# Decoder layer on one core: half of x and the first weights on two queues, and the first four weight chunks applied to both token blocks before their norm factors are known

## The chip, the cores and the metric

The kernel runs on one core of a Trainium2 chip. The metric is the device time of one execution in microseconds (us), as the median of several runs. A profile of one execution gives, per engine, when each instruction ran: PE multiplies matrices (PEld is its loading of the stationary operand), DVE is the vector engine, ACT the scalar engine, POOL is GpSimd, and SP issues transfers.

## The reference

One hybrid decoder layer over x of 256 tokens by 1024 channels, in float32. What matters here is its first sub-layer:

```python
h = h + 0.5 * rmsnorm(swiglu(rmsnorm(h, ffn1_pre_g), ffn1_w_gate, ffn1_w_up, ffn1_w_down), ffn1_post_g)
# rmsnorm(x, g) = x * rsqrt(mean(x*x) + EPS) * g
# swiglu(u)     = (silu(u @ w_gate) * (u @ w_up)) @ w_down
```

Behind it stand a Mamba-2 branch and a differential attention branch beside each other, their gated merge, and a second sub-layer of the same kind. The norm factor r = rsqrt(...) is one number per token, so that it can be applied to a token's row before or after a product with the weights: (r x g) W = r (x g W).

## The kernel before, in words

**Precision.** Every float32 operand of a product is split in two: hi is the operand cast to a rounded 32-bit form, lo is what the cast lost. A product is hi·hi + lo·hi + hi·lo, so each pair of 128-wide tiles costs three matmuls. ACT makes hi (line 167 for weights, 343 and 191 for activations) and DVE makes lo (168, 345, 192).

**Weights** come in chunks of 1 MB through three `raw` buffers (`load_to`, line 140). SP issues the transfers. A buffer is loaded again once DVE has made the last lo of the chunk in it. The first chunk is loaded in four pieces of 256 KB and split in four pieces; chunks 1 to 3 are loaded in halves. `take()` hands out the next split chunk and sees to it that chunks ahead are split.

**Tokens** are two blocks of 128 (block 0 and 1). For a product, x must be transposed (channels on partitions): PE transposes four 128x128 tiles into one PSUM tile `pu`, ACT and DVE read it, multiply by the gain column g, and write hi and lo.

**The start** (lines 263 to 612). ACT issues the transfer of the gain (`stage_f`), SP those of x in four quarters (block 0 halves 0 and 1, block 1 halves 0 and 1), then the weights. PE does six warm-up matmuls (`WARM`) on an identity matrix, transposes the gain (299), transposes both halves of block 0 (340), and does eight more warm-up matmuls (`FILL`). Block 0 goes unscaled, as x·g, into `raw_u`. Block 1 is scaled first: DVE sums its squares (364), POOL makes r1 (330, 331) and multiplies x by it (`un_f`, 373), PE transposes `un_f`, and ACT and DVE write the scaled `u_f`.

**The four first chunks** are w_gate and w_up for the first 512 hidden columns, halves of 512 channels each. `Norm.products` (484) goes through the products (block 0, gate), (block 1, gate), (block 0, up), (block 1, up), two chunks each, twelve matmuls of 128x512 per chunk and block (`mm_nat`, 222), 96 in all. Block 0's results get r0 when they leave PSUM (`evict`, 524). Later products need block 0 scaled too: POOL makes a diagonal matrix of r0 (`dr_f`, 378), PE multiplies it by ones so that r0 stands on every row (`rb_f`, 385), ACT copies that (387), DVE makes the scaled x (`us_f`, 392), and ACT and DVE split it into `u_f` (191, 192). `back` (533) transposes the finished 512 columns of a block (`pt_f`, 537).

**The order.** Inside `own_order` (from line 264 to the `free_order` at the end of `products`) PE, ACT, DVE and SP run in the order in which the program is written; POOL is placed by the scheduler. Behind it the scheduler places all of them. From chunk 4 on (`mm_w`, 206: `pg_f`, `pup_f`) the products are of both blocks at a time.

Of the kernel before, what the change touches and what calls it, by code (L numbers as in the profile page):

```python
# [15 lines left out]
F32R = mybir.dt.float32r  # L16
# [20 lines left out]
RAW_BUFS = 3  # L37
AHEAD = 3
WARM = 6
FILL = 8  # L40
TAIL = 3
BG_US = 3.15
GATE_US = 1.35
# [5 lines left out]
def tile_hybrid_layer(ctx: ExitStack, tc: tile.TileContext, x, ffn1_pre_g, ffn1_w_gate, ffn1_w_up,  # L49
# [19 lines left out]
    def jk(shape, name):  # L69
        return sb.tile(shape, F32, tag="jk", name=name, bufs=2)  # L70
# [12 lines left out]
    def bg(shape, name):  # L83
        return ps.tile(shape, F32, tag="bg", name=name, bufs=5)
# [137 lines left out]
    def mm_nat(acc, w, act, k0, first, last, late):  # L222
# [7 lines left out]
        for i, ((a, b), j) in enumerate(terms):  # L230
            nc.tensor.matmul(acc, a(k0 + j), b(j), start=first and i == 0, stop=last and i == 11)  # L231
# [54 lines left out]
    ones = const.tile([P, P], F32, name="ones")  # L286
    nc.gpsimd.memset(ones, 1.0)

    pw = bg([P, P], "warm")

    def warm(n):

# [2 lines left out]

    warm(WARM)
    cols_f = const.tile([P, KD], F32, name="cols_f")
    pt = bg([P, KD], "pt_cols_f")
    nc.tensor.transpose(pt, stage_f, ident[:KD, :KD])
    nc.vector.tensor_copy(cols_f, pt)  # L300
    cols_a = const.tile([P, P], F32, name="cols_a")
# [31 lines left out]
        return r  # L333

    last_pool = [None]
    def turn(b, q, src, g, to, name):

        pu = bg([P, 4, P], f"pu_{name}{b}{q}")
        for i in range(4):
            nc.tensor.transpose(pu[:, i, :], src[:, i * P:(i + 1) * P], ident)  # L340
        hi, lo = to(q)
        for i in range(4):
            nc.scalar.activation(hi[:, i, :], pu[:, i, :], AF.Identity, scale=g(q * 4 + i))
        for i in range(4):
            nc.vector.scalar_tensor_tensor(lo[:, i, :], pu[:, i, :], g(q * 4 + i), hi[:, i, :].bitcast(F32),
                                           ALU.mult, ALU.subtract)
        return pu

    def in_u(b):
# [8 lines left out]
    def rms(b, tag, eng=None):  # L358

        ss = tiny(2, f"ss_{tag}{b}")  # L360
        for q in range(2):
            src = h[:, b, halves[q]]
            if eng is nc.vector:
                nc.vector.scalar_tensor_tensor(jk([P, 512], f"sq_{tag}{b}{q}"), src, 1.0 / D, src, ALU.mult,
                                               ALU.mult, accum_out=ss[:, q:q + 1])
            else:
                sum_sq(ss[:, q:q + 1], src, 1.0, f"sq_{tag}{b}{q}")
        return rstd_of(ss, 1.0, f"r_{tag}{b}")

    def unit(b, q, r, tag, eng):  # L370
# [7 lines left out]
        last_pool[0] = nc.gpsimd.tensor_scalar(dr, ident, r, None, ALU.mult).ins  # L378
        return dr

    def rescaled(pus, r, g, tag, dr):

        dr = diag(r, tag) if dr is None else dr
        rb = bg([P, P], f"rb_{tag}")
        nc.tensor.matmul(rb, ones, dr, start=True, stop=True)
        rbs = k2([P, P], f"rbs_{tag}")
        nc.scalar.copy(rbs, rb)
        out = []
# [8 lines left out]
    def set_u(us):  # L397
        for q in range(2):
            split(*in_u(0)(q), us[q])

    def post_norm(b, acc, pg, fold, tag):

# [55 lines left out]
    class Norm:  # L458
# [3 lines left out]
        def __init__(self, tag, g):  # L462
            self.tag, self.g, self.pus = tag, g, []
            new_u(tag)
            self.to0 = in_u(0)
            self.dr = None
            self.left = []

        def block0(self):
# [7 lines left out]
        def unit1(self, engs=(nc.vector, nc.vector)):  # L477
            r = rms(1, self.tag)
            self.un = [unit(1, q, r, self.tag, engs[q]) for q in range(2)]

        def turn1(self, q):
            turn(1, q, self.un[q], self.g, in_u(1), self.tag)

        def products(self, ws, evict, at, turns=((0, 0), (0, 1), (1, 0), (1, 1)), late="u"):

            n = 0
            for b, i in turns:
                act = of_block(self.to0 if b == 0 else in_u(1))  # L490
                acc = pj(f"pn_{self.tag}{b}{i}")
                for c in range(2):
                    mm_nat(acc, ws[2 * i + c], act, c * 4, c == 0, c == 1, late if b == 0 else "u")
                    n += 1
                    for f in at.get(n, ()):
                        f()
                if b == 1:
                    evict(b, i, acc, None)
                else:
                    self.left.append(lambda i=i, acc=acc: evict(0, i, acc, self.r0))  # L500
            free_order()

        def turns1(self):
# [7 lines left out]
            self.left.clear()  # L511

        def rescale(self):
            set_u(rescaled(self.pus, self.r0, self.g, self.tag, self.dr))

    def ffn(post_v, tag, norm, ready, turned, then, at, ws=None, **kw):
# [23 lines left out]
        norm.products(ws or [take(1) for _ in range(4)], evict,  # L540
                      {n: [f if f else lambda: back(0) for f in fs] for n, fs in at.items()}, **kw)
# [24 lines left out]


    norm = Norm("f1", lambda j: cols_f[:, j:j + 1])
    raw_u = [k4([P, 4, 2, P], f"raw_u{q}", F32R) for q in range(2)]
    norm.to0 = lambda q: (raw_u[q][:, :, 0, :], raw_u[q][:, :, 1, :])  # L570
    norm.r0 = rms(0, "f1")
    r1 = rms(1, "f1", nc.vector)
    norm.un = [unit(1, q, r1, "f1", nc.gpsimd) for q in range(2)]
    norm.dr = diag(norm.r0, "f1")
    norm.turn0(0)
    for _ in split_steps(False):
        pass
    norm.turn0(1)
    warm(FILL)
    load_to(1 + RAW_BUFS)  # L580

    def gains():
        after_start.append(last_pool[0])
# [9 lines left out]
    def next_norm(tag, name):  # L593
# [9 lines left out]

        return made, ready, lambda: made[0].block0()

    ws = [take(1) for _ in range(2)]
    more = lambda: ws.append(take(1))
    made, ready, turned = next_norm("mx", "mx")
    ffn(ffn1_post_g, "f1", norm, ready, turned, gains,
        {1: [norm.turns1], 2: [more], 4: [norm.settle, more], 5: [norm.rescale], 7: [norm.settle, None]}, ws,  # L610
        turns=((0, 0), (1, 0), (0, 1), (1, 1)), late="w")
    norm = made[0]


# [47 lines left out]
    norm.products([take(1) for _ in range(4)], evict_v,  # L662
                  {3: [norm.turns1], 5: [norm.settle, norm.rescale]})
# [484 lines left out]
    ffn(ffn2_post_g, "f2", norm, store, lambda: None, lambda: None,  # L1148
        {3: [norm.turns1], 5: [norm.settle, norm.rescale], 7: [None]})

    free_order()

# [31 lines left out]
```

## Time and profile before

Median 753.45 us of 3 runs (753.43 to 754.12). The profiled execution took 753.31 us, of which the span from its first to its last instruction is 751.6 us.

| engine | busy us | share of the span |
|---|---|---|
| PE | 742.0 | 99% |
| PEld | 643.8 | 86% |
| DVE | 522.1 | 69% |
| ACT | 437.9 | 58% |
| POOL | 41.0 | 5% |

The granted clock of PE is 0.999 on average. The time from 0 to about 35 us is the start and the four first chunks; it is the only part that the change touches. PE's busy share says that matmuls were in flight, not that they followed each other as closely as they can, so the stage is read from the start times of its rows.

### The profile page before, as it was taken

What the parts mean: (1) busy time and instruction counts of PE and PEld (TensorE: products, weight loads), DVE (VectorE), ACT (ScalarE), POOL (GpSimd) and SP (SyncE); (2) the same over time, 40 slices, a digit from 0 to 9 for tenths busy, and PEclk for the clock granted to TensorE, in tenths of its full rate; (3) what the DMA queues carried; (4) which work ended last, traced back from release to release, by engine and by line L of the source; (5) the groups of instructions that cost most, each with busy time, mean ns of one, the idle gap of its engine ahead of it and who ended that gap; (6) DMA issues with size and microseconds to landing.
All of it is one profiled execution on the core that took longest, in us unless ns stands there. A gap on an engine that the chain in (4) does not pass through costs nothing.

```text
span 751.6 us, 11066 instructions
## 1 busy us (share of the span) xinstructions
PE 742.0 (99%) x4385; PEld 643.8 (86%) x4385; DVE 522.1 (69%) x790; ACT 437.9 (58%) x731; POOL 41.0 (5%) x76
## 2 busy tenths in 40 slices
PE   8999999999999999999999999999999999999996
PEld 7888888888889999898999778788888888888885
DVE  6685667654577888868777987696684867766612
ACT  7475556643565565858867555783563756664511
POOL 7400000000200000000000000000010000000000
PEclk9999999999999999999999999999999999999999
DMA  8685666486253647565556454376371777544701
GB/s 316 158 276 162 222 224 240 181 280 223 64 168 115 203 135 242 169 200 183 161 168 202 166 192 152 129 230 246 112 232 49 225 223 224 177 176 184 275 1 56
DMA packets 94212, 137.96 MB, mean 184 GB/s; under 512 B 2684, under 2 KB 68304, under 8 KB 94160
## 3 DMA queue, kind: packets, MB, share of 16 engines
q1 hardware_dynamic: 91488, 129.51, 52.3%
q0 software_dynamic: 2368, 7.22, 3.2%
q8 instruction: 34, 0.56, 0.3%
q10 hardware_dynamic: 304, 0.53, 0.2%
q14 instruction: 18, 0.15, 0.1%
HBM read 136.17 MB, written 1.08 MB: 183 GB/s over the span
## 4 chain that ended last, share of the span: by engine, by line
PE 96%; DVE 1%; POOL 1%; DMA 1%; ACT 1%; issue 0%; SPq 0%; DVEq 0%; POOLq 0%; ACTq 0%
PE acc_f L433 16%; PE pup_f L216 9%; PE pg_f L216 9%; PE pws L231 6%; PE pgt L231 6%; PE pn_f L231 5%; PE pg_f L215 4%; PE pup_f L215 4%; PE acc_mx L433 3%; PE pn_mx L231 3%; PE pwd L231 3%; PE pxs L204 2%; PE pxs L202 2%; PE pxs L201 2%; PE pz L204 2%; PE pz L201 2%
## 5 line engine op out<-in xcount | busy, mean ns | idle before, releaser
L168 DVE TENSOR_TENSOR wlo<-raw,whi 128x1024 fp32r<-128x1024 f32 (+1 forms) x246 | 291.6, 1213 | 53.6 <-ACT whi L167 50.9
L167 ACT CAST whi<-raw 128x1024 fp32r<-128x1024 f32 (+1 forms) x246 | 247.3, 1044 | 56.7 <-PE acc_f L433 22.7
L216 PE MATMUL pg_f<-u_f,whi 128*128 128x512 f32 x288 | 101.2, 396 | 0.0
L216 PE MATMUL pup_f<-u_f,whi 128*128 128x512 f32 x288 | 101.1, 396 | 0.0
L215 PE MATMUL pg_f<-u_f,wlo 128*128 128x256 f32 x252 | 70.5, 280 | 0.0
L215 PE MATMUL pup_f<-u_f,wlo 128*128 128x256 f32 x252 | 70.3, 279 | 0.0
L216 PEld LDWEIGHTS pg_f<-u_f,whi 128*128 128x128 f32 x288 | 52.9, 188 | 9.8
L216 PEld LDWEIGHTS pup_f<-u_f,whi 128*128 128x128 f32 x288 | 52.7, 188 | 9.8
L433 PE MATMUL acc_f<-whi,gh_f 128*128 128x512 f32 x176 | 58.2, 390 | 0.0
L433 PE MATMUL acc_f<-wlo,gh_f 128*128 128x512 f32 x176 | 58.1, 389 | 0.0
L433 PE MATMUL acc_f<-whi,gl_f 128*128 128x512 f32 x176 | 58.1, 389 | 0.0
L215 PEld LDWEIGHTS pg_f<-u_f,wlo 128*128 128x128 f32 x252 | 47.5, 188 | 1.7
L215 PEld LDWEIGHTS pup_f<-u_f,wlo 128*128 128x128 f32 x252 | 47.5, 189 | 1.6
L220 DVE TENSOR_TENSOR su_f<-pup_f,su_f 128x256 f32<-128x256 f32 x36 | 15.2, 422 | 40.5 <-ACT su_f L219 40.5
L433 PEld LDWEIGHTS acc_f<-wlo,gh_f 128*128 128x128 f32 x176 | 33.0, 188 | 6.9
L433 PEld LDWEIGHTS acc_f<-whi,gl_f 128*128 128x128 f32 x176 | 33.0, 188 | 6.8
L433 PEld LDWEIGHTS acc_f<-whi,gh_f 128*128 128x128 f32 x176 | 33.0, 188 | 6.8
L231 PE MATMUL pgt<-whi,u_mx 128*128 128x512 f32 x128 | 34.8, 400 | 0.0
L201 PE MATMUL pz<-u_mx,whi 128*128 128x256 f32 x128 | 32.3, 288 | 0.0
L219 ACT COPY su_f<-pup_f 128x256 f32<-128x256 f32 x36 | 13.4, 371 | 32.2 <-PE pup_f L216 32.1
L202 PE MATMUL pz<-u_mx,whi 128*128 128x256 f32 x128 | 31.8, 284 | 0.0
L201 PE MATMUL pxs<-u_mx,whi 128*128 128x256 f32 x128 | 31.7, 285 | 0.0
(310 smaller groups left out, 1435.9 us busy)
## 6 DMA issues: line engine op xcount, KB each, us to landing
raw<-in_w_in_dram SPq DMA_DIRECT2D x40, 1024.0 KB, 5.4
raw<-in_ffn_w_down_dram SPq DMA_DIRECT2D x22, 1024.0 KB, 5.0
raw<-in_ffn_w_gate_dram SPq DMA_DIRECT2D x20, 1024.0 KB, 5.7
raw<-in_ffn_w_up_dram SPq DMA_DIRECT2D x20, 1024.0 KB, 5.5
raw<-in_ssd_w_branch_dram SPq DMA_DIRECT2D x8, 1024.0 KB, 5.1
acb<-acd POOLq DMA_DIRECT2D x8, 512.0 KB, 4.9
raw<-in_da_w_branch_dram SPq DMA_DIRECT2D x4, 1024.0 KB, 5.1
raw<-in_w_out_dram SPq DMA_DIRECT2D x4, 1024.0 KB, 5.0
```

The lines of the kernel that those rows point to most:

```text
L167: nc.scalar.copy(hi[:, js, :], r[:, q * nj + j:q * nj + j + n, :])
L168: nc.vector.tensor_sub(lo[:, js, :], r[:, q * nj + j:q * nj + j + n, :], hi[:, js, :].bitcast(F32))
L201: nc.tensor.matmul(acc[m], wh(j)[:, cs], ah(k0 + j), start=first and j == ks[0], stop=False)
L202: nc.tensor.matmul(acc[m], wh(j)[:, cs], al(k0 + j), start=False, stop=False)
L204: nc.tensor.matmul(acc[m], wl(j)[:, cs], ah(k0 + j), start=False, stop=last and j == ks[-1])
L215: nc.tensor.matmul(acc[:, :T], wl(j)[:, cs], ah(j), start=False, stop=False)
L216: nc.tensor.matmul(acc, wh(j)[:, cs], ahl(j), start=j == 0, stop=j == KD - 1)
L219: nc.scalar.copy(dst[:, m, :], acc[:, T:])
L220: nc.vector.tensor_tensor(dst[:, m, :], acc[:, :T], dst[:, m, :], ALU.add)
L231: nc.tensor.matmul(acc, a(k0 + j), b(j), start=first and i == 0, stop=last and i == 11)
L433: nc.tensor.matmul(acc[b][q], x_[:, ts], w_(kt)[:, halves[q]], start=i == 0 and kt == 0 and x_ is ah and w_ is wh, stop=i == n - 1 and kt ...
```

## The change

Constant `FILL` goes from 8 to 2. ACT's queue now issues the first halves of x of both blocks, behind the gain; SP issues the first weight chunk in its four pieces, then the second halves of x, then the other weights. `WARM` and its place stay.

Neither block is scaled before the product: both are transposed unscaled into `raw_u`. A new `mm_both` multiplies one chunk with both blocks, k-tile by k-tile, hi pieces first; all four chunks go through it in the order gate 0, gate 1, up 0, up 1. Both blocks get r when they leave PSUM, and both get the way over `dr_f`, `rb_f`, `rbs`, `us_f` and `u_f`. The squares of block 0 are summed on DVE, those of block 1 on ACT. Two of the four transposes of x, and one of the two `rb_f`, are put between matmuls of a chunk.

```diff
-FILL = 8
+FILL = 2
...
+    def mm_both(accs, w, acts, k0, first, last, between={}):
+        wh, wl = w
+        his = [[(b, a, wh, j) for b in range(2) for a in acts[b]] for j in range(4)]
+        los = [[(b, acts[b][0], wl, j) for b in range(2)] for j in range(4)]
+        terms = his[0] + his[1] + los[0] + his[2] + los[1] + his[3] + los[2] + los[3]
+        for i, (b, x_, w_, j) in enumerate(terms):
+            nc.tensor.matmul(accs[b], x_(k0 + j), w_(j), start=first and j == 0 and w_ is wh and x_ is acts[b][0],
+                             stop=last and j == 3 and w_ is wl)
+            if i + 1 in between:
+                between[i + 1]()
...
     for b in range(2):
-        for q in range(2):
-            nc.sync.dma_start(h[:, b, halves[q]], xv[:, b, halves[q]])
+        nc.scalar.dma_start(h[:, b, halves[0]], xv[:, b, halves[0]])
+    load_to(1)
+    for b in range(2):
+        nc.sync.dma_start(h[:, b, halves[1]], xv[:, b, halves[1]])
     load_to(RAW_BUFS)
...
-    norm.r0 = rms(0, "f1")
-    r1 = rms(1, "f1", nc.vector)
-    norm.un = [unit(1, q, r1, "f1", nc.gpsimd) for q in range(2)]
-    norm.dr = diag(norm.r0, "f1")
-    norm.turn0(0)
-    for _ in split_steps(False):
-        pass
-    norm.turn0(1)
-    warm(FILL)
+    square(ss_f[0], 0, 0, "f1", nc.vector)
+    raised(0, 0)
+    warm(FILL)
+    raised(1, 0)
+    raw(0, 0)
+    steps = split_steps(False)
+    next(steps)
+    raw(1, 0)
+    for _ in steps:
+        pass
     load_to(1 + RAW_BUFS)
...
+    def first_products(evict, back):
+        acts = [of_block(to) for to in raw_to]
+        acc = [[pj(f"pn_f1{b}0") for b in range(2)], None]
+        mm_both(acc[0], take(1), acts, 0, True, False, {16: lambda: raised(0, 1), 20: lambda: raised(1, 1)})
+        square(ss_f[0], 0, 1, "f1", nc.vector)
+        r = [rstd_of(ss_f[0], 1.0, "r_f10")]
+        dr = diag(r[0], "f10")
+        raw(0, 1)
+        raw(1, 1)
+        rb = bg([P, 2, P], "rb_f1")
+        rbs = []
+        w = take(1)
+        rbs.append(on_rows(rb[:, 0, :], dr, "f10"))
+        for q in range(2):
+            square(ss_f[1], 1, q, "f1")
+        r.append(rstd_of(ss_f[1], 1.0, "r_f11"))
+        us = rescaled(pus[0], rbs[0], gain_f, "f10")
+        dr = diag(r[1], "f11")
+        w2 = take(1)
+        mm_both(acc[0], w, acts, 4, False, True, {16: lambda: rbs.append(on_rows(rb[:, 1, :], dr, "f11"))})
+        set_u(0, us)
+        acc[1] = [pj("pn_f101"), bg([P, 512], "pn_f111")]
+        for b in range(2):
+            evict(b, 0, acc[0][b], r[b])
+        us = rescaled(pus[1], rbs[1], gain_f, "f11")
+        mm_both(acc[1], w2, acts, 0, True, False)
+        w = take(1)
+        set_u(1, us)
+        mm_both(acc[1], w, acts, 4, False, True)
+        split_to(5)
+        for b in range(2):
+            evict(b, 1, acc[1][b], r[b])
+        free_order()
+        back(0)
```

`raised(b, q)` transposes one half of one block, `raw(b, q)` writes its hi and lo with the gain, `square` sums the squares of one half, `diag` and `on_rows` put a factor on every row, `rescaled` and `set_u` make the scaled operand. Behind chunk 3 the order of the instructions on every engine is that of before, but for a few around the two `pt_f` transposes.

More of the change, by code (lines that the diff above doesn't have):

```diff
@@ L287, in tile_hybrid_layer @@
     nc.gpsimd.memset(ones, 1.0)
-    pw = bg([P, P], "warm")
+    pw = pj("warm")[:, :P]
     def warm(n):
@@ L340, in turn, with gained @@
             nc.tensor.transpose(pu[:, i, :], src[:, i * P:(i + 1) * P], ident)
-        hi, lo = to(q)
+        return pu
+    def gained(pu, q, g, hi, lo):
         for i in range(4):
@@ L346, in turn @@
                                            ALU.mult, ALU.subtract)
+    def turn(b, q, src, g, to, name):
+        pu = transposed(b, q, src, name)
+        gained(pu, q, g, *to(q))
         return pu
@@ L356, in of_block, with square, rms @@
         return lambda j: parts[j // 4][0][:, j % 4, :], lambda j: parts[j // 4][1][:, j % 4, :]
-    def rms(b, tag, eng=None):
+    def square(ss, b, q, tag, eng=None):
+        src = h[:, b, halves[q]]
+        if eng is nc.vector:
+            nc.vector.scalar_tensor_tensor(jk([P, 512], f"sq_{tag}{b}{q}"), src, 1.0 / D, src, ALU.mult,
+                                           ALU.mult, accum_out=ss[:, q:q + 1])
+        else:
+            sum_sq(ss[:, q:q + 1], src, 1.0, f"sq_{tag}{b}{q}")
+    def rms(b, tag):
         ss = tiny(2, f"ss_{tag}{b}")
         for q in range(2):
[L362 to L367, printed above, removed]
+            square(ss, b, q, tag)
         return rstd_of(ss, 1.0, f"r_{tag}{b}")
@@ L379, in diag, with on_rows @@
         return dr
-    def rescaled(pus, r, g, tag, dr):
-        dr = diag(r, tag) if dr is None else dr
-        rb = bg([P, P], f"rb_{tag}")
+    def on_rows(rb, dr, tag):
         nc.tensor.matmul(rb, ones, dr, start=True, stop=True)
@@ L387, in rescaled @@
         nc.scalar.copy(rbs, rb)
+        return rbs
+    def rescaled(pus, rbs, g, tag):
         out = []
@@ L395, in rescaled, with set_u @@
         return out
-    def set_u(us):
+    def set_u(b, us):
         for q in range(2):
-            split(*in_u(0)(q), us[q])
+            split(*in_u(b)(q), us[q])
     def post_norm(b, acc, pg, fold, tag):
@@ L465, in __init__ @@
             self.to0 = in_u(0)
-            self.dr = None
             self.left = []
@@ L475, in turn0, with unit1, products @@
             self.pus.append(turn(0, q, h[:, 0, halves[q]], self.g, self.to0, self.tag))
-        def unit1(self, engs=(nc.vector, nc.vector)):
+        def unit1(self):
             r = rms(1, self.tag)
-            self.un = [unit(1, q, r, self.tag, engs[q]) for q in range(2)]
+            self.un = [unit(1, q, r, self.tag, nc.vector) for q in range(2)]
         def turn1(self, q):
             turn(1, q, self.un[q], self.g, in_u(1), self.tag)
-        def products(self, ws, evict, at, turns=((0, 0), (0, 1), (1, 0), (1, 1)), late="u"):
+        def products(self, evict, at):
+            ws = [take(1) for _ in range(4)]
             n = 0
-            for b, i in turns:
+            for b in range(2):
                 act = of_block(self.to0 if b == 0 else in_u(1))
[L491 to L500, printed above, removed]
+                for i in range(2):
+                    acc = pj(f"pn_{self.tag}{b}{i}")
+                    for c in range(2):
+                        mm_nat(acc, ws[2 * i + c], act, c * 4, c == 0, c == 1, "u")
+                        n += 1
+                        for f in at.get(n, ()):
+                            f()
+                    if b == 1:
+                        evict(b, i, acc, None)
+                    else:
+                        self.left.append(lambda i=i, acc=acc: evict(0, i, acc, self.r0))
             free_order()
@@ L513, in rescale, with ffn @@
         def rescale(self):
-            set_u(rescaled(self.pus, self.r0, self.g, self.tag, self.dr))
-    def ffn(post_v, tag, norm, ready, turned, then, at, ws=None, **kw):
+            rbs = on_rows(bg([P, P], f"rb_{self.tag}"), diag(self.r0, self.tag), self.tag)
+            set_u(0, rescaled(self.pus, rbs, self.g, self.tag))
+    def ffn(post_v, tag, ready, turned, then, products):
         gu = []
@@ L538, in back @@
             split(gh[:, :, bs], gl[:, :, bs], pt_)
-        norm.products(ws or [take(1) for _ in range(4)], evict,
-                      {n: [f if f else lambda: back(0) for f in fs] for n, fs in at.items()}, **kw)
+        products(evict, back)
         back(1)
@@ L565, in ffn @@
         mm_n(acc, gu, done, turned)
-    norm = Norm("f1", lambda j: cols_f[:, j:j + 1])
-    raw_u = [k4([P, 4, 2, P], f"raw_u{q}", F32R) for q in range(2)]
-    norm.to0 = lambda q: (raw_u[q][:, :, 0, :], raw_u[q][:, :, 1, :])
-    norm.r0 = rms(0, "f1")
-    r1 = rms(1, "f1", nc.vector)
-    norm.un = [unit(1, q, r1, "f1", nc.gpsimd) for q in range(2)]
-    norm.dr = diag(norm.r0, "f1")
-    norm.turn0(0)
-    for _ in split_steps(False):
-        pass
-    norm.turn0(1)
-    warm(FILL)
+    new_u("f1")
@@ new lines, in tile_hybrid_layer, with raised, raw @@
+    raw_u = [[k4([P, 4, 2, P], f"raw_u{b}{q}", F32R) for q in range(2)] for b in range(2)]
+    raw_to = [lambda q, b=b: (raw_u[b][q][:, :, 0, :], raw_u[b][q][:, :, 1, :]) for b in range(2)]
+    gain_f = lambda j: cols_f[:, j:j + 1]
+    pus = [[None] * 2 for _ in range(2)]
+    ss_f = [tiny(2, f"ss_f{b}") for b in range(2)]
+    def raised(b, q):
+        pus[b][q] = transposed(b, q, h[:, b, halves[q]], "f1")
+    def raw(b, q):
+        gained(pus[b][q], q, gain_f, *raw_to[b](q))
+    square(ss_f[0], 0, 0, "f1", nc.vector)
@@ L580, in tile_hybrid_layer @@
+    raised(0, 0)
[6 more added lines that the diff above has]
+    for _ in steps:
+        pass
     load_to(1 + RAW_BUFS)
+    def first_products(evict, back):
[28 more added lines that the diff above has]
+        split_to(5)
+        for b in range(2):
+            evict(b, 1, acc[1][b], r[b])
+        free_order()
+        back(0)
@@ L604, in next_norm @@
         return made, ready, lambda: made[0].block0()
-    ws = [take(1) for _ in range(2)]
-    more = lambda: ws.append(take(1))
     made, ready, turned = next_norm("mx", "mx")
-    ffn(ffn1_post_g, "f1", norm, ready, turned, gains,
-        {1: [norm.turns1], 2: [more], 4: [norm.settle, more], 5: [norm.rescale], 7: [norm.settle, None]}, ws,
-        turns=((0, 0), (1, 0), (0, 1), (1, 1)), late="w")
+    ffn(ffn1_post_g, "f1", ready, turned, gains, first_products)
     norm = made[0]
@@ L660, in evict_v @@
             nc.scalar.activation(vt[c][:, b, :], acc, AF.Identity, scale=r)
-    norm.products([take(1) for _ in range(4)], evict_v,
-                  {3: [norm.turns1], 5: [norm.settle, norm.rescale]})
+    norm.products(evict_v, {3: [norm.turns1], 5: [norm.settle, norm.rescale]})
     wdt = k2([P, KD, H_SSD], "wdt")
@@ L1147, in tile_hybrid_layer @@
     norm = made[0]
-    ffn(ffn2_post_g, "f2", norm, store, lambda: None, lambda: None,
-        {3: [norm.turns1], 5: [norm.settle, norm.rescale], 7: [None]})
+    ffn(ffn2_post_g, "f2", store, lambda: None, lambda: None, lambda evict, back: norm.products(
+        evict, {3: [norm.turns1], 5: [norm.settle, norm.rescale], 7: [lambda: back(0)]}))
     free_order()
```

4 lines of the change are left out of this document (2 added, 2 removed).

## The prediction

> **What bounds the kernel now.** I read the page first: engines' busy time and the chain that ended last.
>
> ```profile
> PE 742.0 (99%) x4385; PEld 643.8 (86%) x4385; DVE 522.1 (69%) x790; ACT 437.9 (58%) x731; POOL 41.0 (5%) x76
> ...
> PE 96%; DVE 1%; POOL 1%; DMA 1%; ACT 1%; issue 0%; SPq 0%; DVEq 0%; POOLq 0%; ACTq 0%
> ```
>
> PE is the chain for 96% of the span. Behind chunk 3 the instructions and their order stay as they were, so the change is worth the amount by which it moves the moment at which PE enters chunk 4, nothing else. Next I read the timeline of the first 35 us (start, duration, engine, line, operation, tiles, count, and in brackets the idle time before it with what ended it).
>
> ```profile
> 4.66 1.60 PE L340 MATMUL pu_f<-ident,h 128*128 128x128 f32 x8
> ...
> 5.81 1.14 ACT L343 ACTIVATE raw_u<-pu_f,cols_f 128x128 fp32r<-128x128 f32 x4 [0.52 <-PE pu_f L340]
> ...
> 7.36 0.62 ACT L167 CAST whi<-raw 128x512 fp32r<-128x512 f32 x1 [0.41 <-DMA raw<-in_ffn_w_gate_dram]
> ...
> 8.03 0.73 PE L231 MATMUL pn_f<-whi,raw_u 128*128 128x512 f32 x2
> ...
> 12.76 2.65 POOL L378 TENSOR_SCALAR dr_f<-ident,r_f 128x128 f32<-128x128 f32 x1
> ...
> 13.24 2.09 PE L231 MATMUL pn_f<-whi,raw_u 128*128 128x512 f32 x8
> ...
> 19.70 1.07 PE L231 MATMUL pn_f<-wlo,u_f 128*128 128x512 f32 x4
> 20.61 1.07 PE L231 MATMUL pn_f<-whi,u_f 128*128 128x512 f32 x4
> ...
> 33.13 0.62 PE L216 MATMUL pg_f<-u_f,whi 128*128 128x512 f32 x2
> ```
>
> Four matmuls start 0.91 us behind four others (19.70 to 20.61): 0.228 us each. The 96 of the four chunks need 21.9 us. They begin at 8.03, because the first weight piece landed only at 7.3 (the cast waited for it). The first twelve take until 12.1 (2.7 us of work, 1.3 of waiting for casts), eight transposes take until 13.24, and from there to 33.13 there are 84 matmuls (19.2 us), one `rb_f` (0.15) and one `pt_f` (0.4): no wait is left. So **at most 8.03 us of start and 1.3 us of waits can be won**; what comes after 13.24 is full.
>
> **The change, part by part.** All sums are against the profiled execution (753.31 us, of it 751.6 span), which stands 0.14 us under the median of 753.45; I add the difference to the median.
>
> *Transfers.* In the DMA view the four quarters of x, issued by SP at 0.80, 1.22, 1.69 and 2.16, land after 2.7, 3.3, 3.6 and 4.5 us, so at 3.5, 4.5, 5.3 and 6.7; the first weight piece at 7.3. Now weights come first on SP and land long before they are cast. x of block 0 goes behind the gain on ACT's queue, whose issue takes 0.60 from 0.79, so it is issued at 1.4. Its landing is not in this trace. Best: 1.4 + 2.7 = 4.1. Worst: as the third transfer in all, 5.3. I take 4.8, in the middle, since two queues feed it beside the first weight pieces. Block 1's half is then between 4.9 and 7.3 (fifth transfer); it is needed at 7. All later bytes come in the same sum as before and have more slack.
>
> The page "DMA: Bandwidth & Descriptors" of the Trainium skill, section "Issuing engines are not separate DMA queues", speaks against a gain: a second issuing engine saves issue time only, the transfers run on the same 16 engines and interleave. The trace had moved 721 KB by 4.5 us and 904 KB by 5.0, and landings came some 0.5 us behind their bytes; three quarter-MB transfers that share this alike are 786 KB, so by that rule x would land near 5.2 and the sum be 0.4 us more.
>
> *The first matmul.* PE's gate on transposes is not x alone: `pu_f` started at 4.66 right behind the gain's transpose, though x had landed at 3.5. So they start at 4.66 at the earliest, at 4.85 by my landing. ACT started 1.15 after the first (4.66 to 5.81): now **6.0**. Four gain steps take ACT 1.0 (10.46 to 11.46, the last result 0.13 later), a cast of 512 columns 0.63 (three in 1.9). The first cast is done at 7.63, the first matmul starts at **7.7** instead of 8.03: 0.35 won, and no more, because the cover of the late weights goes and what is late next is x itself.
>
> *Chunk 0.* The second matmul group needs block 1's lo. ACT: block 0's hi 6.0 to 7.0, cast 7.63, block 1's hi 8.63 (8.76). DVE (1.04 per four lo, 0.68 per quarter of a weight chunk): 7.18, 8.22, 8.9; then block 1's lo, of which the first is there at 9.25. PE does three matmuls by 8.4 and waits to 9.3: **0.95 of wait**. Thirteen matmuls run to 12.27, the transposes of x's second halves (0.4 each) follow at 12.27 and 13.58, and the chunk ends at 14.9, the first `rb_f` at 15.05. Its factor is early: DVE's sum of squares at 12.6, then 0.95 + 0.8 on POOL.
>
> *Chunk 1.* On ACT its casts stand behind the second halves' hi, which stand behind PE's transposes. From a transpose group to ACT it took 0.64 (568.35 to 568.99). So ACT runs 12.91 to 13.91 and 14.22 to 15.22, and the first cast of 1024 columns (1.05) is done at 16.27. PE waits from 15.05 to 16.3: **1.25 of wait**; before, ACT had those casts ready. Sixteen matmuls later, at 19.98, PE meets the second `rb_f` in its own order. It needs r1: ACT's second cast (17.33), the copy (0.24), two sums of squares (563.33 to 564.72: 1.4) end at 18.97; POOL's r takes from 564.82 to 565.75 and the diagonal 0.79 there, so it is ready at 20.8. PE waits to 20.87: **0.9 of wait**, with eight matmuls and chunks 2 and 3 queued behind it.
>
> The diagonal's duration decides here, and the trace has two:
>
> ```profile
> 12.76 2.65 POOL L378 TENSOR_SCALAR dr_f<-ident,r_f 128x128 f32<-128x128 f32 x1
> ...
> 201.25 0.79 POOL L378 TENSOR_SCALAR dr_mx<-ident,r_mx 128x128 f32<-128x128 f32 x1
> ...
> 565.75 0.79 POOL L378 TENSOR_SCALAR dr_f<-ident,r_f 128x128 f32<-128x128 f32 x1
> ```
>
> The long one lay beside DVE's L168 (12.66 to 15.0, weights and hi, both from SBUF) and ended just behind it, while DVE had gone on to L345 (one PSUM operand). From 18.75 to 20.8 DVE does the scaled x (L392, also one PSUM operand), so I take 0.79; the upper end is 2.65.
>
> *Chunks 2 and 3.* 0.15 for `rb_f`, then 56 matmuls at 0.228, from 21.0 to **33.8**. No wait is left: ACT has chunk 3's casts by 26.2, DVE its lo by 28.9 and chunk 4's by 32.5, the bank of the sixth product is free at 19.8, and chunk 3's transfer (issued when DVE leaves chunk 0 at 12, 5.7 to land) at 18. POOL loses two products of 2.08 each that nothing replaces on the path.
>
> *What moves behind 33.13.* Before, one `pt_f` (0.4) was inside the 33.13; now both come behind it, the second waiting for DVE's eviction (0.7 each, first at 33.8, second done at 35.3). Counted to the same instruction behind `pt_cols` this adds 0.2. DVE and ACT then split chunk 5 by 40 and PE needs it at 41, so nothing further.
>
> *Sum.* Earlier start −0.35; waits 0.95 + 1.25 + 0.9 = 3.1 against 1.3; transposes 0.8 against 1.15, one `rb_f` more, one `pt_f` moved out, and some 0.2 of small gaps in before's rows: entering chunk 4 at 33.8 against 33.13, and 0.2 behind it, **+0.9 us**. 753.45 + 0.9 = 754.35, say **754.4**. That is 0.12% and inside 0.2% (1.5 us), which is about what a measurement of this kernel can tell from no change.
>
> **Rivals.**
>
> *PE's clock, the slower side.* The granted clock is 1.00 in every early slice, yet the first twelve warm-up records (two per matmul) start 0.22 apart and the sixteen from 6.0 on 0.117: a first phase at 1.9 times the time, until about 5.9. Before, eight `FILL` matmuls kept PE full until 7.9 and products followed; now PE works 1.2 us between 6.0 and 9.3. If that leaves it in, or returns it to, the slow phase until the thirteenth matmul or so, 12 to 15 matmuls cost 0.2 more each: +2.4 to +3.0 on the sum, 757.1. Against it: in the last slices the clock stays 1.00 to 749 and is 0.50 from 750, five us after the last matmul at 744.9, and the gaps here are 1.3 at most. It decides if gaps of one us count.
>
> The page "TensorE: Matmul & The Clock Gate", section "What's actually happening", has the full clock given after a busy window of some 3.4 us and taken after an idle one; by that the gaps here are too short, and the trace's end agrees.
>
> *POOL blocked at the second diagonal, also slower.* 2.65 in place of 0.79 at 20.0 puts 1.85 us straight onto PE: 754.35 + 1.85 = 756.2. It decides if L392 hinders POOL, or if DVE is late and in L168 there.
>
> *x late on ACT's queue.* Landing at 5.3 or beyond, or block 1's half behind 7, moves everything by 0.5 to 1.0: 754.9 to 755.4.
>
> *The waits of chunk 1 don't come, the faster side.* If ACT gets the transposes and sums sooner than my steps (1.25 and 0.9 gone), 754.35 − 2.15 = 752.2. Nothing in the rows allows it, since ACT's order is written out.
>
> **How the numbers follow.** My forecast 58% (753.7 to 754.9), x late 15%, POOL 12%, clock 10%, no waits in chunk 1 5%. The range leaves out the clock and the faster case and takes in POOL's bound: 753.5 to 756.4. Slower by over 1.5 us: POOL 12, clock 10 and half of x late, 30%. Faster by over 1.5: a part of the last case and what I overlooked, 4%. Within: 66%.
>
> **What would show it.** In the profile after: the first L241 matmul at 7.7; a hole in PE before the fourth; PE idle of about 1.25 ended by ACT's cast of chunk 1, and of 0.9 ended by POOL at the second `rb_f`; `pg_f` at 33.8. Wrong would be: `pg_f` before 33, `dr_f` of 2 us or more, or early matmuls 0.43 apart.

## The result, and the profile after

The changed kernel takes **757.11 us** (median of 6 executions, 755.59 to 757.97) against 753.91 for the kernel before beside it: a ratio of 1.0039, 95% interval 1.0026 to 1.0052. It is slower by 3.2 us. The forecast was 754.4, its range 753.5 to 756.4, counted from 753.45 for the kernel before. (A second set of nine executions, below, has 755.76, inside that range. The six executions here lie 2.4 us apart, those of the kernel before 1.0.) The profiled execution of the changed kernel took 757.28 us, of it 755.6 span, so it is 3.97 us behind the profiled execution of before.

First the page: the engines' busy time and the chain that ended last.

```profile
PE 744.0 (98%) x4375; PEld 645.0 (85%) x4375; DVE 524.7 (69%) x800; ACT 438.0 (58%) x734; POOL 33.4 (4%) x75
...
PE 95%; DVE 1%; ACT 1%; DMA 1%; issue 0%; POOL 0%; ACTq 0%; DVEq 0%; POOLq 0%
```

PE is still the chain, with a point less of the span. Its busy time rose by 2.0 us though it does ten records fewer: some of its instructions took longer. The page does not say which, so next comes the timeline of the start (columns as before: start, duration, engine, line, operation, tiles, count, and in brackets the idle time with what ended it).

```profile
4.45 0.27 PE L315 MATMUL pt_cols_f<-ident,stage_f 8*128 8x8 f32 x1
...
5.55 1.11 PE L355 MATMUL pu_f<-ident,h 128*128 128x128 f32 x4 [0.84 <-DMA h<-in_x_dram]
...
6.71 1.14 ACT L361 ACTIVATE raw_u<-pu_f,cols_f 128x128 fp32r<-128x128 f32 x4 [3.14 <-PE pu_f L355]
7.72 0.63 ACT L167 CAST whi<-raw 128x512 fp32r<-128x512 f32 x1
...
7.80 1.11 PE L355 MATMUL pu_f<-ident,h 128*128 128x128 f32 x4 [0.28 <-DMA h<-in_x_dram]
...
8.57 1.63 PE L241 MATMUL pn_f<-whi,raw_u 128*128 128x512 f32 x3
...
10.53 2.50 PE L241 MATMUL pn_f<-whi,raw_u 128*128 128x512 f32 x5 [0.34 <-DVE raw_u L363]
...
12.83 1.05 PE L241 MATMUL pn_f<-wlo,raw_u 128*128 128x512 f32 x2
...
14.81 0.63 POOL L405 TENSOR_SCALAR dr_f<-ident,r_f 128x128 f32<-128x128 f32 x1
...
15.48 0.60 PE L355 MATMUL pu_f<-ident,h 128*128 128x128 f32 x4
...
18.21 0.38 PE L410 MATMUL rb_f<-dr_f,ones 128*128 128x128 f32 x2
...
19.61 2.14 PE L241 MATMUL pn_f<-whi,raw_u 128*128 128x512 f32 x8 [1.01 <-ACT whi L167]
...
23.06 0.62 POOL L405 TENSOR_SCALAR dr_f<-ident,r_f 128x128 f32<-128x128 f32 x1
...
23.74 0.49 PE L410 MATMUL rb_f<-dr_f,ones 128*128 128x128 f32 x2 [0.17 <-POOL dr_f L405]
...
36.78 0.39 PE L216 MATMUL pg_f<-u_f,whi 128*128 128x512 f32 x1
```

Three things are to be seen. The weight cast at 7.72 no longer waits for a transfer, as it did before; now the transposes wait for x, twice (5.55 and 7.80). The five matmuls at 10.53 are followed by the next at 12.83: 0.46 each, where the eight at 19.61 take 1.98 to the next row (21.59): 0.25 each. And `pg_f`, the entry into chunk 4, is at 36.78 against 33.13: 3.65 of the 3.97 us are lost by then.

The chain of the first 42 us (start, duration, what) says where that begins:

```profile
0.79 0.58 ACTq L281
1.41 0.37 ACTq L287
1.81 5.95 DMA h<-in_x_dram
7.80 1.13 PE pu_f L355 x4
```

ACT's queue issues the gain (L281), then block 0's half of x at 1.41 and block 1's at 1.81. The latter takes 5.95 us to land, and everything up to the fourth matmul hangs on it. By the DMA view block 0's half takes 4.1 (it lands at 5.5).

Set against the terms of the prediction, the way to `pg_f` splits like this:

| stretch | forecast | measured | difference |
|---|---|---|---|
| to the fourth matmul (block 1's operand) | 9.3 | 10.53 | +1.23 |
| from there to the first `rb_f` | 5.6 | 7.68 | +2.08 |
| to chunk 1's first matmul (wait for the cast) | 1.4 | 1.40 | 0 |
| to the second `rb_f` (wait for the diagonal) | 4.57 | 4.13 | −0.44 |
| to `pg_f` | 12.93 | 13.04 | +0.11 |
| sum | 33.8 | 36.78 | +2.98 |

So the miss has two parts: late operands of x, and slow matmuls in chunk 0. The first thirteen matmuls from 10.53 take 4.95 us to the transposes at 15.48; at 0.228 they would take 2.97.

### The profile page after: what moved, and what is told of

The parts are those of the page before. It is cut to its first block, busy times and chain, and to the rows that moved or that the text cites. A ratio compares the mean times of both kernels' runs of the same rounds, so it can differ in the third digit from the quotient of the medians.

```text
span 755.6 us, 11056 instructions
## 1 busy us (share of the span) xinstructions
PE 744.0 (98%) x4375; PEld 645.0 (85%) x4375; DVE 524.7 (69%) x800; ACT 438.0 (58%) x734; POOL 33.4 (4%) x75
## 4 chain that ended last, share of the span: by engine, by line
PE 95%; DVE 1%; ACT 1%; DMA 1%; issue 0%; POOL 0%; ACTq 0%; DVEq 0%; POOLq 0%
PE acc_f L462 16%; PE pup_f L216 9%; PE pg_f L216 9%; PE pws L231 6%; PE pgt L231 6%; PE pg_f L215 4%; PE pup_f L215 4%; PE pn_f L231 3%; PE acc_mx L462 3%; PE pn_mx L231 3%; PE pwd L231 3%; PE pn_f L241 2%; PE pxs L204 2%; PE pxs L202 2%; PE pxs L201 2%; PE pz L204 2%
## 5 line engine op out<-in xcount | busy, mean ns | idle before, releaser
L168 DVE TENSOR_TENSOR wlo<-raw,whi 128x1024 fp32r<-128x1024 f32 (+1 forms) x246 | 291.1, 1211 | 55.4 <-ACT whi L167 52.7
L201 PE MATMUL pxs<-u_mx,whi 128*128 128x256 f32 x128 | 31.7, 285 | 0.0
L202 PE MATMUL pxs<-u_mx,whi 128*128 128x256 f32 x128 | 31.4, 283 | 0.0
```

The lines of the kernel that those rows point to most:

```text
L168: nc.vector.tensor_sub(lo[:, js, :], r[:, q * nj + j:q * nj + j + n, :], hi[:, js, :].bitcast(F32))
L201: nc.tensor.matmul(acc[m], wh(j)[:, cs], ah(k0 + j), start=first and j == ks[0], stop=False)
L202: nc.tensor.matmul(acc[m], wh(j)[:, cs], al(k0 + j), start=False, stop=False)
```

## Experiments

The theory after the result was this: x lands late because it shares the transfers with weights that started ahead of it; PE therefore stands idle from 4.7 to 5.5, before it has reached its full pace, and this idle time keeps it at the slow pace for nearly all of chunk 0. The rivals were: late x alone costs everything and the pace is an accident of one execution; or the new order of the products costs the time. Every ratio is against runs of the kernel before on the same chip.

### x_first: x ahead of the weights

```diff
-        nc.scalar.dma_start(h[:, b, halves[0]], xv[:, b, halves[0]])
+        nc.sync.dma_start(h[:, b, halves[0]], xv[:, b, halves[0]])
```

SP issues x's first halves at 0.80, before the weights; all else is the changed kernel.

> The changed kernel, but SP alone issues all: the first halves of x of both blocks, then the first weight chunk, then the rest; ACT issues only the gain. Theory LATE X (x on a second queue shares the transfer engines with the weights and lands 2 us later than alone; that alone sets the loss): the first halves land at 3.5 and 4.5, transposes start at 4.65, the gain steps at 5.8 and block 1's behind the first cast at 7.4; chunk 4 begins 2.3 us sooner than the 36.8 of the changed kernel, time about 754.8. Theory SLOW PE (the clock is what costs): if PE's first phase still lasts until 14.8, the matmuls of chunk 0 stay 0.43 apart and only 0.5 is won, 756.5; if an unbroken start lets the phase end at 5.9 as in the kernel before, the two gains add up: chunk 4 at 33.6, time about 754.5 or less, with all matmuls 0.228 apart.

Measured: 754.02 (753.51 to 754.12), ratio 1.0000 [0.9991, 1.0009]. The whole loss is gone. PE in its timeline:

```profile
4.65 1.11 PE L355 MATMUL pu_f<-ident,h 128*128 128x128 f32 x4
...
9.09 1.43 PE L241 MATMUL pn_f<-whi,raw_u 128*128 128x512 f32 x5 [0.51 <-DVE raw_u L363]
...
16.31 2.11 PE L241 MATMUL pn_f<-whi,raw_u 128*128 128x512 f32 x8 [1.01 <-ACT whi L167]
...
20.44 0.49 PE L410 MATMUL rb_f<-dr_f,ones 128*128 128x128 f32 x2 [0.21 <-POOL dr_f L405]
...
33.48 0.39 PE L216 MATMUL pg_f<-u_f,whi 128*128 128x512 f32 x1
```

The transposes start without a wait, and five matmuls take 1.43 where they took 2.50. The two waits of chunk 1 are still there, at 16.31 and 20.44, where the prediction has 16.3 and 20.87, and `pg_f` comes at 33.48 (forecast 33.8). With x in time the prediction's sum holds nearly row by row. What is left of the change, the new order of the products included, is together worth nothing that the median shows; no run takes the order alone.

### cover_gap and cover_all: x as late as in the change, the idle time filled

```diff
-    pw = pj("warm")[:, :P]
+    pw = bg([P, P], "warm")
...
     nc.vector.tensor_copy(cols_f, pt)
+    warm(2)
```

Two more warm-up matmuls (into a bank of their own pool) stand between the gain's transpose and the transposes of x. The transfers stay as in the change. `cover_all` has, besides, `FILL = 4` and two warm-up matmuls before the fourth product.

> The changed kernel with two more warm-up matmuls (four records) between the gain's transpose and the first transpose of x, so that PE works through the 0.9 us in which it waits for x; transfers as changed. SLOW PE: the pace goes to full at about 6 as in the kernel before, chunk 0's matmuls come at 0.228, 1.8 us won: 755.3. LATE X: nothing changes, 757.1, as PE waits for x at the same places. If the pace is full at 6 but lost again in the holes of chunk 0, the first matmuls are at 0.228 and later ones at 0.43.

Measured: 755.29 (754.72 to 755.68), ratio 1.0018 [1.0009, 1.0027].

```profile
4.65 1.22 PE L310 MATMUL warm<-ident 128*128 128x128 f32 x4
5.67 1.06 PE L356 MATMUL pu_f<-ident,h 128*128 128x128 f32 x4
...
8.13 0.66 PE L356 MATMUL pu_f<-ident,h 128*128 128x128 f32 x4 [0.85 <-DMA h<-in_x_dram]
...
10.41 1.43 PE L241 MATMUL pn_f<-whi,raw_u 128*128 128x512 f32 x5 [0.67 <-DVE raw_u L364]
```

The transposes of x are no earlier than in the change (5.67 and 8.13 against 5.55 and 7.80), yet the same five matmuls take 1.43. Thirteen take 3.08 (10.41 to 13.49) against 4.95. In the profiled executions these two fills, work that nothing uses, give back 2.0 us of the span (755.6 to 753.6). In medians it is 1.8 against the first set of the change (757.11) and 0.5 against the second (755.76): what disappears is the upper part of the change's spread, up to 757.97, while no execution here is over 755.68. What is left against x_first, 1.3 us, is the late x.

> As the run with the covered wait, and four instead of two warm-up matmuls between the two transposes of x, and two more ahead of the fourth matmul of chunk 0: PE has no hole over 0.6 us from 1.6 on. SLOW PE: full pace from about 6 to the end, 755.3 at the latest, and all executions alike. LATE X: 757.1, or 0.2 more for the added work ahead of block 1's transpose.

Measured: 755.14 (754.55 to 755.74), ratio 1.0017 [1.0008, 1.0025]: no different from cover_gap. In cover_gap the warm-up matmuls at 6.52 end at the full pace (the last two start 0.11 apart), and PE then idles for 0.85 and 0.67; filling such gaps gained nothing more.

### before_fill2: the eight fills of the kernel before cut to two

```diff
-FILL = 8
+FILL = 2
```

> The kernel before with FILL at 2 instead of 8, nothing else. PE then stands idle from about 6.5 to 8.0 with the first products behind. SLOW PE: if full pace, once given at 5.9, is lost by a hole of 1.5 us, or is not yet given, chunk 0 runs at 0.43 and the time is 1 to 2 us more, 755 to 756; if it is given at 5.9 and holes of this size do not matter, 753.9 as before. LATE X says 753.9.

Measured: 754.05 (753.40 to 756.12, eleven executions, of which two, 755.11 and 756.12, stand apart), ratio 1.0005 [0.9996, 1.0014].

```profile
6.36 0.61 PE L294 MATMUL warm<-ident 128*128 128x128 f32 x4
8.46 2.72 PE L231 MATMUL pn_f<-whi,raw_u 128*128 128x512 f32 x8 [1.49 <-ACT whi L167]
```

PE is idle for 1.49 us before the first product, a longer hole than the change's 0.84. But the four matmuls ahead of it took 0.61 (0.11 apart), so the full pace was there before the hole, and the first matmuls from 11.01 start 0.23 apart. The median shows no cost; what the two slower executions did, no profile shows.

### gain_on_sp: two queues kept, with x at the head of its own

```diff
-    nc.scalar.dma_start(stage_f, ffn1_pre_g[0].rearrange("(c p) -> c p", p=P))
+    nc.sync.dma_start(stage_f, ffn1_pre_g[0].rearrange("(c p) -> c p", p=P))
```

> The changed kernel with the gain's transfer ahead of the weights on SP, so that ACT's queue starts with x at 0.8 as SP's did before. SHARING (two queues share the transfer engines): x lands 3.6 to 4.1 after its issue as in the changed kernel, so block 0's half at 4.4 to 4.9 and block 1's at 6.6 to 7.2; transposes start at 4.65 to 4.95, the first at hardly any hole, so PE's pace goes to full near 6: 754.5. If only the late issue of 1.4 was at fault, it lands at 3.5 as from SP, and block 1's at 4.5, and the time is that of the run with x first, 754.0.

Measured: 754.03 (753.59 to 754.11), ratio 0.9999 [0.9990, 1.0007]. Here the expectation of my theory was missed. x is issued at 0.80 and 1.21 and lands at 3.8 and 5.5, though the weights start at 1.25 beside it; the weight pieces land at 5.25 to 7.4. Two queues as such did no harm: what cost the change its time was that the gain's issue (0.58 us) stood ahead of x on ACT's queue and gave the weights a head start. A second reading comes from PE:

```profile
6.05 0.60 PE L355 MATMUL pu_f<-ident,h 128*128 128x128 f32 x4
7.51 0.96 PE L241 MATMUL pn_f<-whi,raw_u 128*128 128x512 f32 x3 [0.86 <-ACT whi L167]
9.03 1.43 PE L241 MATMUL pn_f<-whi,raw_u 128*128 128x512 f32 x5 [0.56 <-DVE raw_u L363]
```

A hole of 0.86, as long as the change's 0.84, and the matmuls behind it are at full pace: by then it had been reached (the transposes at 6.05 took 0.60 for four, not 1.11).

### after_again: the changed kernel once more

Nothing is edited.

> The changed kernel once more, for the spread of its executions: the six so far lay at 755.6 (two) and 756.9 to 758.0 (four). SLOW PE: the moment at which the pace goes to full differs between executions of one program, so two groups 1.5 to 2 apart come again, and if the profiled one is of the quicker group, its chunk 0 has matmuls 0.228 apart from an earlier one on. LATE X alone would give one group.

Measured: 755.76 (754.79 to 757.34, nine executions), ratio 1.0024 [1.0015, 1.0034]. The executions spread evenly over 2.5 us, not in two groups as I expected. The profiled one took 756.99 and again had `pu_f` late (5.29, 0.57 idle for x) and matmuls 0.43 apart until 13.8. x_first spread over 0.6 us. A slow phase that ends at another moment in each execution would fit this spread; only the profiled two show where it ended.

### x_first_hole and hole_no_fill: idle time with x in time

The converse was still to be made: x early, and idle time before the full pace. The first attempt cuts x_first's warm-up, the second cuts its fills too.

```diff
-WARM = 6
+WARM = 3
...
-FILL = 2
+FILL = 0
```

(The second pair is in `hole_no_fill` alone.)

> x_first (x issued before the weights, 754.02) with three warm-up matmuls in place of six, so that PE runs dry before its full pace is given though x is in time. IDLE BEFORE THE PACE (theory): the transposes move up to about 3.7, and PE then idles some 1.5 to 2 us between them and the first product at about 7.5; the products of chunk 0 start 0.43 apart, pg_f falls behind 35 and the median is 755.5 to 757. LATE X ALONE (rival): the pace is 0.228 by the first products as in x_first, nothing on the path changes, 754.0, or a little less if the first product comes earlier.

Measured: 753.10 (752.87 to 754.95), ratio 0.9992 [0.9983, 1.0001], `pg_f` at 32.58. Neither theory was put to the test, since no hole came about:

```profile
3.17 0.27 PE L315 MATMUL pt_cols_f<-ident,stage_f 8*128 8x8 f32 x1
3.66 1.11 PE L355 MATMUL pu_f<-ident,h 128*128 128x128 f32 x4 [0.22 <-DMA h<-in_x_dram]
...
6.51 3.13 PE L241 MATMUL pn_f<-whi,raw_u 128*128 128x512 f32 x8
```

With six warm-up matmuls PE was not free until 4.45, though gain and x had landed; with three the whole start is 1.0 us earlier (products from 6.51 against 7.51), fills and transposes follow each other, and 0.9 us arrives in the median (0.6 by the ratios; the two kernels ran on different chips). Two of the eleven executions, 754.18 and 754.95, stand apart.

> x_first_hole (three warm-up matmuls, x issued before the weights; 753.10, pg_f 32.58, products from 6.51 and at 0.23 apart from about 8) without its two fills, so that PE stands idle for about 1 us, from 5.4 to 6.5, before its full pace is given, with x in time. IDLE BEFORE THE PACE (theory): the products of chunk 0 start 0.43 apart until about 12, pg_f near 34 and the median 754.3 to 755.3, with more spread. LATE X ALONE (rival): the pace comes by about 8 as before, pg_f 32.6, 753.1.

Measured: 754.32 (753.84 to 756.26), ratio 1.0006 [0.9998, 1.0015]; its profiled execution took 755.24.

```profile
3.60 1.97 PE L355 MATMUL pu_f<-ident,h 128*128 128x128 f32 x8 [0.16 <-DMA h<-in_x_dram]
6.46 4.02 PE L241 MATMUL pn_f<-whi,raw_u 128*128 128x512 f32 x8 [0.88 <-ACT whi L167]
10.27 1.05 PE L241 MATMUL pn_f<-wlo,raw_u 128*128 128x512 f32 x2
```

The first product is no later than in x_first_hole (6.46 against 6.51), x is in time, and PE has 0.88 of idle before it. Now eight matmuls take 3.81 to the next row, against 2.97, and they stay 0.43 apart until 12.8; `pg_f` falls from 32.58 to 34.65. The median pays 1.2 us (1.1 by the ratios, again on different chips) for two fills left out. Idle time before the full pace costs without any late x. Nor is the slow pace an accident of one execution: the three traces with idle time of 0.57 or more before the full pace have matmuls 0.43 apart until 12.8 or later, the eleven others have the full pace by 8.6 at the latest. The executions spread over 2.4 us, as those of the change do.

### rb_late, turns_early, turns_gain, turns_warm3: the two waits of chunk 1

```diff
-{16: lambda: rbs.append(on_rows(rb[:, 1, :], dr, "f11"))}
+{24: lambda: rbs.append(on_rows(rb[:, 1, :], dr, "f11"))}
```

`rb_late` is x_first with the second `rb_f` behind the last matmul of chunk 1.

> The run with x first, with the second diagonal product behind the last matmul of chunk 1 instead of its 16th. CHAIN: only the second wait (0.6 us) goes, 753.4. ENGINE LOAD: it comes back in chunk 3 or at chunk 4, since block 1's scaled operand is then later, 754.0.

Measured: 753.40 (752.95 to 753.58), ratio 0.9991 [0.9982, 1.0000]. The second wait is gone, the first (before chunk 1) stays: 0.6 us.

```diff
-{16: lambda: raised(0, 1), 20: lambda: raised(1, 1)}
+{8: lambda: raised(0, 1), 12: lambda: raised(1, 1)}
```

`turns_early` is x_first with the transposes of the second halves eight matmuls earlier; `turns_gain` is gain_on_sp with the same; `turns_warm3` is turns_early with `WARM = 3`.

> The run with x first, with the transposes of the second halves of x put behind the 8th and 12th matmul of chunk 0 instead of the 16th and 20th. In that run PE waits 1.2 us ahead of chunk 1 for ACT's cast and 0.6 ahead of the second diagonal product. Theory CHAIN (these waits hang on the place of the two transposes, since the casts stand behind the gain steps on ACT): ACT's cast of chunk 1 is done at 14.2, before PE ends chunk 0 at 14.9, the second factor at 18.7, both waits go, 1.8 us won: 752.2, faster than the kernel before by 0.2%. Rival ENGINE LOAD (ACT and DVE have too much work in this stage wherever it stands): the wait comes back at another matmul, less than 0.5 won, 753.6.

Measured: **752.22** (751.71 to 752.28), ratio 0.9975 [0.9965, 0.9985].

```profile
14.54 0.39 PE L410 MATMUL rb_f<-dr_f,ones 128*128 128x128 f32 x2
14.68 2.07 PE L241 MATMUL pn_f<-whi,raw_u 128*128 128x512 f32 x8
...
18.41 0.38 PE L410 MATMUL rb_f<-dr_f,ones 128*128 128x128 f32 x2
...
31.37 0.39 PE L216 MATMUL pg_f<-u_f,whi 128*128 128x512 f32 x1
```

No bracket stands behind chunk 1's first matmuls nor behind either `rb_f`: one move of PE's transposes took both waits, since ACT's casts, copy and squares all stood behind them in ACT's order.

> Two queues kept (the gain on SP, so that x starts on ACT's queue at 0.80, as in gain_on_sp, 754.03) with the two transposes of the second halves behind matmuls 8 and 12 of chunk 0, as in turns_early. ADDITIVE (theory): the two waits of chunk 1 go, as they did there (1.8 us): 752.2, pg_f near 31.4. If the waits came back because the weights land 1 us later than in x_first or the second halves of x later, 753 to 754. The early transposes need x's second halves at about 10.5.

Measured: 752.28 (751.80 to 752.35), ratio 0.9975 [0.9966, 0.9984]; `pg_f` at 31.77. The gain of turns_early stays when x comes on a queue of its own.

> turns_early (752.22, pg_f 31.37) with three warm-up matmuls in place of six. The start goes 1 us earlier, as in x_first_hole (first product 6.51 in place of 7.51, 0.9 off the median there). ADDITIVE: pg_f 30.4, 751.3. If the cover of the transposes or the weights of chunk 1 are late at the earlier time, a wait comes back and the median is 752.2.

Measured: **751.42** (751.16 to 751.56, five executions), ratio 0.9965 [0.9951, 0.9978]. It is faster than both kernels of the change, by 2.6 us against before.

## Why the prediction was wrong, point by point

- **What bounds the kernel** held: little changed behind chunk 3, and 3.65 of the 3.97 us are there at `pg_f`.
- **The landing of x was mis-sized, in its bounds too.** Block 0's half landed at 5.5, not 4.8 and outside 4.1 to 5.3; block 1's at 7.76, not within 4.9 to 7.3. (In the three other traces with these transfers, after_again, cover_gap and cover_all, it was 5.2 to 5.7 and 7.5 to 8.1.) I counted x as the third transfer in a row, and left out that all that is issued meanwhile takes its share: the second piece, issued earlier, landed at 4.7, and pieces 3 and 4, issued at 1.71 and 2.17, at 7.5 and 8.2, in step with x. The page "DMA: Bandwidth & Descriptors" of the Trainium skill, section "Issuing engines are not separate DMA queues", says that transfers of all issuing engines interleave on the same 16 engines; the trace agrees, and the 5.2 worked out by that rule was nearer than my 4.8. Yet gain_on_sp shows that who starts first decides as well: with x at 0.80 on ACT's queue it landed at 3.8 beside the weights. This term, up to the fourth matmul, measured +1.23 in the profile; in medians, cover_gap against x_first, 1.3 us. It is the rival "x late on ACT's queue": both of its conditions came, and its price of 0.5 to 1.0 was too low.
- **The wait before the fourth matmul** came by the mechanism forecast (DVE's lo of block 1), but 1.2 later, since ACT got block 1's transposes only at 8.95 and not at 7.63.
- **The step that failed is the pace of chunk 0**: "Thirteen matmuls run to 12.27", at 0.228 each. They ran at 0.43 for nine of thirteen, +1.98 in the profile; in medians 1.8 us in the first set of the change and 0.5 in the second, both against cover_gap. The prediction had this as a rival at 10% with the price 2.4 to 3.0, and rejected it by the end of the program, where the clock column keeps 1.00 for five us after the last matmul. That row tells how the full pace is lost; the question here was when it is given. (It is no firm bound for the loss either: in turns_early the clock is at 0.50 from 745.70, 2.2 us after the last matmul.) gain_on_sp (a hole of 0.86 after it) and after or hole_no_fill (0.84 and 0.88 before it) have the same hole with opposite results. I also kept the two rivals apart, "x late" and "clock", with a price for each, when the first brings about the second: late x is what makes PE idle between 4.7 and 5.5. So the range left out the case in which both hold, which is the one that came.
- **Luck plays in on both sides.** The clock rival's 757.1 is the median of the first set, but by another sum: 2.7 for the clock and nothing for late x. And the second set's 755.76 lies inside the range, though the sum behind the range has the landing of x and the pace wrong in that set too. Late x alone, as in cover_gap (755.29), would have stayed within the range; the pace is what can take the time out of it.
- **When the pace is given** can be read more closely. Each kept trace holds a record of the full clock. The column does not show where it starts, since it prints 1.00 also where there is no record. The record begins at 5.74 us in before, 6.82 in cover_gap and 7.80 in x_first, but at 14.55 in the change, 13.99 in after_again and 12.91 in hole_no_fill: there the spacing changes. It lasts 744.11, 740.69 or 737.28 us in all fourteen traces, lengths that lie 3.41 apart. So, as far as fourteen lengths tell, the clock is given and taken in steps of 3.41 us, and the steps begin at another moment in each execution. The section "What's actually happening" of the page "TensorE: Matmul & The Clock Gate" (Trainium skill) has two windows: an idle one that takes the full clock and a busy one of some 3.4 us that gives it, free-running, not starting with the work. The traces agree with the second, by their steps of 3.41; I used the first to judge a case of the second.
- **Which idle time counted** follows in part. Counted back from 14.55, the change has 1.04 us of idle PE in the step from 4.31 to 7.73, 0.41 in the next and none in the last. The hole of 0.84 was thus not alone: the step behind it, with the wait of 0.34 for block 1's lo, did not give the full clock either. Both waits come of late x. In thirteen of the fourteen traces the full clock begins behind the first step with at most 0.03 us idle; rb_late, with 0.51 idle in its step, is the exception.
- **The wait of 1.25 for chunk 1's cast** was right: 18.21 to 19.61 less 0.15 for `rb_f`. x_first has it too.
- **The wait at the second `rb_f`** was right in kind, 0.5 instead of 0.9. The diagonal took 0.63 at 14.81 with DVE idle and 0.62 at 23.06 beside DVE's scaled x (L421, 21.97 to 24.1), not 0.79 and not 2.65: the rival "POOL blocked" fell.
- **Chunks 2 and 3** were right: 12.80 from 23.98 to `pg_f`, as forecast. What moves behind it cost 0.3, not 0.2.
- **The rival on the faster side**, waits gone, needed another order, as the prediction said; with that order turns_early has its 752.2. The equal number is partly luck: 1.8 us came off x_first's 754.02, not 2.15 off 754.35.

What stays open: how much idle time a step may hold (0.26 in x_first_hole, from 1.56 to 4.97, held the full clock back, rb_late's 0.51 did not), and whether the slower executions of one kernel are those whose steps begin at a bad moment. That would fit, since the starts of the steps differ between executions, but only the profiled executions show theirs.

## What to carry to other kernels

When an edit shortens the warm-up or the fill of PE, or lets it wait for a transfer in its first microseconds, look where in the trace matmuls of one shape change from one spacing to the other, and ask whether the new idle time lies before that point: there a hole of 0.9 us cost some 1.2 us in the median and 2 in the profiled execution (hole_no_fill), while behind it holes of 0.5 to 0.9 did not slow the matmuls that followed (gain_on_sp, cover_gap). When two rivals are written down, ask whether one of them causes the other, and price both together. And when a stage has waits on an engine whose order is written out, move what that engine is waiting for, not the instruction that shows the wait: two transposes moved by eight matmuls took away 1.8 us of waits.

## What the runs showed of the hardware

- The granted clock column stayed at 1.00 in the early slices of every run, while matmuls of 128x512 were 0.43 apart until 14.5 in the change and 0.228 afterwards. The spacing shows the first phase, the column does not: the trace's own record of the full clock begins at 14.55 there, and the column prints 1.00 where there is no record.
- The full clock lasted 744.11, 740.69 or 737.28 us in the fourteen traces: it is given and taken in steps of 3.41 us, which begin at another moment in each execution.
- The moment of the full pace differs between executions with the same start: four transposes from 4.61 to 4.66 took 1.11 in x_first and gain_on_sp, 0.81 in turns_early and 0.66 in rb_late.
- x's first half (256 KB) on ACT's queue took 4.1 us to land when issued 0.6 us behind SP's first weight piece (the change; 3.7 to 4.2 in the three other traces with these transfers), 3.0 when issued 0.45 us ahead of it (gain_on_sp), and 2.8 on SP's queue ahead of all weights (x_first). The head start decided here; a queue of its own gained nothing.
- POOL's diagonal from SBUF took 0.62 beside DVE's scaled x, which has one operand in PSUM, and 2.65 in before beside DVE's L168 with both in SBUF. The page "SBUF — State Buffer" of the Trainium skill, section "Who interferes with whom", has that distinction for DVE and GpSimd; the traces agree.
